# A third raw weight buffer in the down projection, operand loads of the quarter-size products on GpSimd's queue, and the seven products in another order

## The chip, the cores and the metric

The kernel runs on one core of one Trainium2 chip. The metric is the device time of one execution in microseconds (us); lower is better. Before the change three runs took 1799.60, 1798.85 and 1799.17 us, a median of 1799.17 us.

A core has five engines with instruction streams of their own, which wait for each other by semaphores: TensorE (PE, matrix products), VectorE (DVE), ScalarE (ACT), GpSimd (POOL) and SyncE (SP), which here only issues transfers (DMA). Each engine works strictly through its own list, so an instruction that waits holds back all that stand behind it.

## The reference

One step of a one-layer streaming encoder on 1056 tokens (1024 of a prompt and 32 of a sample group), in float32, with a model width of 1024: windowed attention with sinks beside a gated short convolution, cross-attention into 256 memory tokens, and a squared-ReLU MLP, each added to the residual, then a final RMS norm.

```python
x = x + (sigmoid(ga) * a + sigmoid(gb) * bo) @ w_mix_out
...
x = x + co @ w_co
hm = rms_norm(x, g_mlp)
x = x + jnp.square(jax.nn.relu(hm @ w_up)) @ w_down
...
y_prompt = rms_norm(xp, norm_final_g)
```

The change touches only the product with `w_down`, whose weight has 4096 rows and 1024 columns.

## The kernel before, in words

**Products.** Every float32 product is made from three passes of TensorE in its reduced float type: weight and operand are each split into a high part and the remainder, and high·high, high·low and low·high are added. For a weight a transfer of 512 KB brings 128x1024 values into a raw buffer `wr` (issued by SP, L164), ACT casts it to `wh` (L131), and DVE subtracts to get `wl` (L132). There are two raw buffers, and three of `wh` and of `wl`. A raw buffer is free for the next load when its `wl` is done. `next_w` keeps the casts of the two following weights issued ahead of a product (`LOOK = 2`). The third raw buffer that `fetch_w` knows (`third`, named `wr3`) is used in other parts of the kernel and is cleared before the down part.

**The down part.** It is the last 385 us. The product with `w_down` is made by a scheme of Strassen's kind: seven products of half the tokens (528) by half the depth and half the width, instead of eight. They are called b11, b21, t2, n4, n3, n1 and b22. The operand sums were written to DRAM earlier (`b_d`, `t_d`, `n_d` and so on in the trace), and for weight sums too (`wsum_d`). A product comes in one of two forms.

- `stage` (b11, t2, n3, n1, b22): eight items, each with one weight and 2 x 24 matmuls of 128x128 by 128x264 (L1923 to L1925). The results of a pair of items are added to the residual x1 by `to_x1` (L1907), 12 DVE instructions for each of four column groups in b11, 9 in t2, 6 in n3 and n1. Sixteen operands of 128x528 are loaded by SP (`fetch_op`, L1670, 264 KB each) and split by ACT (L1355) and DVE (L1356).
- `stage2` (b21 and n4): the product is divided once more into seven quarter-size products P1, P6, P2, P7, P5, P4, P3, so fourteen items of 24 matmuls (L2100 to L2102), each with one weight. Their operands are prepared during the stage before (`prepare`). For each k of eight, `fetch_two` loads two operands, POOL makes three sums (`first_sums`, L1701 to L1703), ACT and DVE split two results (`first_split`, L1708 and L1709), and later one more sum is split whole (`extra_split`, L1712 and L1713). The results are combined on ACT, DVE and POOL (L2051, L2053, L2058, L1905). At the end of a `stage2` SP loads the operands of the stage that follows: twelve transfers during its last nine items, four more with the first item of the next stage.

**What sets the order.** A scheduler places the instructions of each engine by rules of its own and by the order in which the program records them; `pin` holds an instruction at its recorded place. Stages are recorded in the order in which they are called. In a stage that comes after, or prepares, a `stage2`, the items run in the order `paired`, where two column groups advance together; in the others a column group is finished before the next begins.

**Names in the order listings.** `Ga` and `Gb` are residual tiles, `acc2` accumulators, `wl_...` remainders of a weight with a running number, `H`, `n1`, `n3`, `n4`, `t2`, `b22`, `Z`, `lt` are places for operands, and `ct` is scratch.

Of the kernel before, what the change touches and what calls it, by code (L numbers as in the profile page):

```python
# [10 lines left out]
F32 = mybir.dt.float32  # L11
# [29 lines left out]
def hybrid_step(ctx: ExitStack, tc: tile.TileContext, io):  # L41
    nc = tc.nc
    act, dve, pool_e, pe, sp = nc.scalar, nc.vector, nc.gpsimd, nc.tensor, nc.sync
# [11 lines left out]
    def closed(cm):  # L55
        cm.__exit__(None, None, None)
# [42 lines left out]
    def pin(ins):  # L99
        return tc.keep_in_program_order(ins)  # L100
# [49 lines left out]
    third = {}  # L150
# [137 lines left out]
    W = {}  # L288
# [1348 lines left out]


    dn, wanted2, coming2 = {}, [], []
    KINDS = ["b11", "b21", "t2", "n4", "n3", "n1", "b22"]  # L1640
    after2 = [KINDS[KINDS.index(kind) + 1] for kind in RAW2]


# [24 lines left out]
    def fetch_op(kind, k):  # L1668
        hi, lo = take_pair(kind, k)
        sp.dma_start(lo.bitcast(F32), op_d[kind][:, k])  # L1670
        return hi, lo
# [17 lines left out]
    two = {}  # L1689

    def fetch_two(kind, k):
        fetch_op(kind, k)
        two["x", k] = lo = take_slot((kind, 8 + k, 1))
        two["r", k] = take_slot((kind, "r", k), F32)
        sp.dma_start(lo.bitcast(F32), op_d[kind][:, 8 + k])

    def first_sums(kind, k):

# [16 lines left out]
    def extra_split(kind, k):  # L1715
        cut(*take_pair(kind, ("e", k)), two["r", k])
# [23 lines left out]
    def open_down():  # L1740
        flush()
        closed(L["cm"])
        closed(L["cm2"])
        S["h"] = ctx.enter_context(tc.tile_pool(name="hpool", bufs=1, reuse_waits="tile"))


# [72 lines left out]
    at = {}  # L1819
# [168 lines left out]
    def prepare(kind):  # L1988

        at = {n: [] for n in range(8)}  # L1990
        for n in range(4):
            for k in (2 * n, 2 * n + 1):
                at[n].append(lambda k=k: fetch_two(kind, k))
                at[n + 1].append(lambda k=k: first_sums(kind, k))
                at[n + 2].append(lambda k=k: first_split(kind, k))
        for k in range(8):
            at[6 + k // 4].append(lambda k=k: extra_split(kind, k))
        return at

    def stage(kind, w, then, q=None, each=None, more=None):  # L2000
        nxt = KINDS.index(kind) + 1
        at = prepare(KINDS[nxt]) if nxt < len(KINDS) and KINDS[nxt] in RAW2 else None
        order = paired if at or kind in after2 else steps
        if nxt < len(KINDS) and not at:
            item(lambda: wanted2.extend((KINDS[nxt], k) for k in range(16)))
        for n, (j, t) in enumerate(order):

            def fn(ws, n=n, j=j, t=t):
                prod(kind, j, t, then, q)(ws)
                if nxt < len(KINDS) and all(x[1] != t for x in order[n + 1 :]):  # L2010
                    drop_pairs(kind, range(8 * t, 8 * t + 8))
                pump2(4 if n == 0 and kind in after2 else 0 if at else 3)
                for x in at[n] if at else ():
                    x()
                if behind and (j, t) == (1, 0):
                    behind.pop()()

            item(fn, (*w, j, t))
            if each and t:
                item(lambda j=j: each(j))  # L2020
            if more and (j, t) == (1, 0):
                item(more)
        if nxt < len(KINDS):
            item(lambda: pump2(0))

    def stage2(kind, h, f0, last):
# [61 lines left out]
        n = 0  # L2088
        for p in order:
            for i in range(2):  # L2090

                def fn(w, p=p, i=i, n=n):
                    wh, wl = w
                    if i == 0 and p in start:
                        banks[into[p]] = wide_tile()
                    a = banks[into[p]][:, i, :QT]
                    for k in range(8):
                        hi, lo = operand2(kind, p, k)
                        s = slice(k * P, k * P + P)
                        pe.matmul(a, wh[:, s], hi, start=(p in start and k == 0), stop=False, skip_group_check=True)  # L2100
                        pe.matmul(a, wh[:, s], lo, start=False, stop=False, skip_group_check=True)  # L2101
                        pe.matmul(a, wl[:, s], hi, start=False, stop=(k == 7), skip_group_check=True)  # L2102
                    if i:
                        ended_with(p)
                    after(p, i)
                    beside(n)

                item(fn, weights[p](i))
                n += 1

    stage("b11", ("w_down", 0), ((*A12, True, False), (*A21, False, False), (*A22, False, False), (*A11, True, False)))
    stage2("b21", *A11, True)
    stage("t2", ("w_sum", 0), ((*A12, False, False), (*A21, True, False), (*A22, True, False)))
    stage2("n4", *A21, False)
    stage("n3", ("w_sum", 2), ((*A21, True, True), (*A22, True, False)))
    stage("n1", ("w_sum", 3), ((*A22, False, True), (*A12, True, False)), more=lambda: final(0))
    item(lambda: gained(2, range(4, 8)))
    stage("b22", ("w_sum", 1), ((*A12, True, True),), q=0)
# [121 lines left out]
```

## Time and profile before

| what | value |
|---|---|
| runs | 1799.60, 1798.85, 1799.17 us; median 1799.17 |
| the profiled execution | 1795.82 us, its span 1794.0 us, 1.82 us around it |
| PE busy | 1741.9 us (97% of the span) |
| DVE, ACT, POOL busy | 1269.9 (71%), 881.9 (49%), 756.5 us (42%) |
| loads and stores by SP's and ACT's queues | 296.37 MB, 49.7% of what 16 DMA engines could take in the span |
| by POOL's queue | 70.46 MB, 11.5% |

PE is busy nearly all the time, so the idle time of PE, and stretches in which it steps at half its clock, are what can be won. Both are concentrated in the down part, from about 1409 us on. Matmuls overlap in the trace: each is listed with 0.28 us, but the next begins 0.12 us later. At the lower clock the step is 0.22 us.

### The profile page before, as it was taken

The page shows a single profiled execution, that of the slowest core. Times are in us where ns is not written, and L with a number is a line of the kernel's source. Part 1 is how long each engine was busy: PE and PEld are TensorE (multiplying, and loading weights), DVE is VectorE, ACT ScalarE, POOL GpSimd, SP SyncE. Part 2 cuts the span into 40 slices and gives each one's busy share as a digit, 9 for nine tenths or more (in the row PEclk, how much of TensorE's full clock was granted, in tenths as well). Part 3 has the DMA queues.
Part 4 walks back from the last instruction along what each step waited for, and adds up shares of the span by engine and source line. Part 5 has one row for each costly group of instructions (what it writes and reads, how often), then busy time and mean ns, then how long its engine had stood idle before and what let it go on. Part 6 is the DMA issues. An engine that isn't in the chain of part 4 may idle for free. (4 is left out here: it accounts for less than half of the span.)

```text
span 1794.0 us, 32861 instructions
## 1 busy us (share of the span) xinstructions
PE 1741.9 (97%) x12166; PEld 1716.5 (96%) x12166; DVE 1269.9 (71%) x2322; ACT 881.9 (49%) x1716; POOL 756.5 (42%) x869
## 2 busy tenths in 40 slices
PE   9999999999999999999999999999999988989998
PEld 8999999999999999999999999999999988988998
DVE  7776877768766647646777877776666776875775
ACT  8643535435345334335565756754444444443543
POOL 0016586664664655543233240026555441731121
PEclk9999999999999999999999999999999998999999
DMA  4334445455556888877756675766666837548544
GB/s 181 108 105 139 157 162 179 162 186 177 181 182 239 293 286 281 289 253 256 260 193 212 223 241 183 271 207 216 217 221 221 315 113 227 192 132 289 195 143 156
DMA packets 191056, 369.70 MB, mean 206 GB/s; under 512 B 19616, under 2 KB 108352, under 8 KB 190768
## 3 DMA queue, kind: packets, MB, share of 16 engines
q1 hardware_dynamic: 169840, 296.37, 49.7%
q0 software_dynamic: 20432, 70.46, 11.5%
q8 instruction: 96, 1.57, 0.4%
q10 hardware_dynamic: 624, 0.77, 0.1%
q14 instruction: 64, 0.52, 0.1%
HBM read 265.41 MB, written 101.53 MB: 205 GB/s over the span
## 5 line engine op out<-in xcount | busy, mean ns | idle before, releaser
L131 ACT CAST wh<-wr 128x1024 fp32r<-128x1024 f32 (+1 forms) x226 | 236.1, 1045 | 360.9 <-PE acc L206 80.8
L132 DVE TENSOR_TENSOR wl<-wr,wh 128x1024 fp32r<-128x1024 f32 (+1 forms) x226 | 303.5, 1344 | 108.7 <-ACT wh L131 107.5
L205 PE MATMUL acc<-X,wh 128*128 128x384 f32 (+1 forms) x864 | 282.0, 326 | 0.2 <-ACT X L284 0.2
L206 PE MATMUL acc<-X,wh 128*128 128x384 f32 (+1 forms) x864 | 279.1, 323 | 0.2 <-DVE X L285 0.2
L207 PE MATMUL acc<-X,wl 128*128 128x384 f32 (+1 forms) x864 | 278.2, 322 | 0.0
L206 PEld LDWEIGHTS acc<-X,wh 128*128 128x128 f32 x864 | 162.9, 189 | 1.6 <-DVE X L285 0.5
L205 PEld LDWEIGHTS acc<-X,wh 128*128 128x128 f32 x864 | 162.6, 188 | 1.3 <-ACT X L284 0.6
L207 PEld LDWEIGHTS acc<-X,wl 128*128 128x128 f32 x864 | 162.6, 188 | 0.1
L281 POOL TENSOR_TENSOR xacc<-xacc,ct 128x384 f32<-128x384 f32 (+1 forms) x56 | 72.4, 1296 | 207.9 <-ACT ct L279 206.1
L205 PE MATMUL acc<-Y,wh 128*128 128x384 f32 (+1 forms) x432 | 140.2, 325 | 4.8 <-DVE ct L1093 3.4
L206 PE MATMUL acc<-Y,wh 128*128 128x384 f32 (+1 forms) x432 | 139.5, 323 | 0.4 <-DVE Y L816 0.4
L207 PE MATMUL acc<-Y,wl 128*128 128x384 f32 (+1 forms) x432 | 139.4, 323 | 0.4 <-DMA wl<-wl_d 0.4
L762 POOL TENSOR_TENSOR xacc<-xacc 128x256 f32<-128x256 f32 x132 | 115.0, 871 | 29.4 <-DMA xacc<-in_w_down 22.4
L762 POOL TENSOR_TENSOR ws<-ws 128x256 f32<-128x256 f32 x132 | 111.2, 842 | 26.6 <-DMA ws<-in_w_down 19.0
L131 ACT CAST PTh<-pt 128x512 fp32r<-128x512 f32 (+3 forms) x94 | 45.8, 516 | 102.2 <-PE pt L603 101.0
L205 PEld LDWEIGHTS acc<-Y,wh 128*128 128x128 f32 x432 | 81.2, 188 | 6.2 <-DVE ct L1093 4.3
L206 PEld LDWEIGHTS acc<-Y,wh 128*128 128x128 f32 x432 | 81.2, 188 | 1.0 <-DVE Y L816 1.0
L207 PEld LDWEIGHTS acc<-Y,wl 128*128 128x128 f32 x432 | 81.2, 188 | 0.7 <-DMA wl<-wl_d 0.7
L589 ACT ACTIVATE S<-S,nmx 128x257 f32<-128x257 f32 (+1 forms) x132 | 64.2, 488 | 25.7 <-DVE nmx L584 24.6
L905 PE MATMUL acc<-n,wh 128*128 128x264 f32 x256 | 72.9, 285 | 1.0 <-DVE Z L1572 1.0
L907 PE MATMUL acc<-n,wl 128*128 128x264 f32 x256 | 73.1, 285 | 0.0
L906 PE MATMUL acc<-n,wh 128*128 128x264 f32 x256 | 72.9, 285 | 0.0
(622 smaller groups left out, 5855.1 us busy)
## 6 DMA issues: line engine op xcount, KB each, us to landing
wr<-in_w_up SPq DMA_DIRECT2D x53, 512.0 KB, 4.6
wr<-in_w_in SPq DMA_DIRECT2D x52, 512.0 KB, 4.1
wr<-wsum_d SPq DMA_DIRECT2D x40, 512.0 KB, 3.5
wr<-in_w_conv_out SPq DMA_DIRECT2D x24, 512.0 KB, 4.3
wr<-in_w_mix SPq DMA_DIRECT2D x24, 512.0 KB, 4.5
wr<-in_w_down SPq DMA_DIRECT2D x20, 512.0 KB, 3.7
n_d<-Z SPq DMA_DIRECT2D x32, 264.0 KB, 4.3
xacc<-in_w_down POOLq DMA_DIRECT2D x16, 512.0 KB, 4.0
```

The lines of the kernel that those rows point to most:

```text
L131: act.copy(hi, src)
L132: dve.tensor_sub(lo, src, hi.bitcast(F32))
L205: pe.matmul(out, wh[:, a], hi, start=(k == 0), stop=False)
L206: pe.matmul(out, wh[:, a], lo, start=False, stop=False)
L207: pe.matmul(out, wl[:, a], hi, start=False, stop=(k == len(acts) - 1))
L281: pool_e.tensor_tensor(acc, acc, sq, op=ALU.add)
L589: act.activation(stl[:, h, : nk + 1], stl[:, h, : nk + 1], AF.Exp, scale=-1.0, bias=nmx[:, h : h + 1], accum_out=den[:, h : h + 1],)
L762: pin(pool_e.tensor_tensor(t[:, to], t[:, x], t[:, y], op=op))
L905: pe.matmul(acc, wh[:, a], hi, start=(start and k == 0), stop=False, skip_group_check=True)
L906: pe.matmul(acc, wh[:, a], lo, start=False, stop=False, skip_group_check=True)
L907: pe.matmul(acc, wl[:, a], hi, start=False, stop=(k == 3), skip_group_check=True)
```

## The change

Six edits, all in the down part.

1. The order of the seven products is b11, t2, b21, n3, n4, n1, b22 instead of b11, b21, t2, n4, n3, n1, b22. So b21 is prepared during t2 (before: b11) and n4 during n3 (before: t2), and each `stage2` is followed by n3 and n1 (before: t2 and n3). The marks of which addition is the last on a tile move with it, so that the sums of squares of the tiles of A21 follow n4.
2. `fetch_two` issues its two loads on POOL's queue instead of SP's, and pins them. There are 16 of them in each preparation, 32 in all.
3. `open_down` gives `fetch_w` a third raw buffer, in memory that is free by then; every third weight of the down part goes there.
4. The eight calls of `extra_split` are spread over three items as 2, 3, 3 instead of over two as 4, 4; so those of k = 0, 1 and 4 are recorded one item earlier.
5. In `stage2`, the casts of the next weight are recorded directly after the matmuls of an item, ahead of that item's combinations and splits (`issue_w()`), so one weight further ahead.
6. The calls at the end stand in the new order.

```diff
-    KINDS = ["b11", "b21", "t2", "n4", "n3", "n1", "b22"]
+    KINDS = ["b11", "t2", "b21", "n3", "n4", "n1", "b22"]
...
     def fetch_two(kind, k):
-        fetch_op(kind, k)
+        pin(pool_e.dma_start(take_pair(kind, k)[1].bitcast(F32), op_d[kind][:, k]))
         two["x", k] = lo = take_slot((kind, 8 + k, 1))
         two["r", k] = take_slot((kind, "r", k), F32)
-        sp.dma_start(lo.bitcast(F32), op_d[kind][:, 8 + k])
+        pin(pool_e.dma_start(lo.bitcast(F32), op_d[kind][:, 8 + k]))
...
         closed(L["cm2"])
+        third.update(n=0, pool=W["pool"])
...
         for k in range(8):
-            at[6 + k // 4].append(lambda k=k: extra_split(kind, k))
+            at[5 + (k + 1) // 3].append(lambda k=k: extra_split(kind, k))
...
                         pe.matmul(a, wl[:, s], hi, start=False, stop=(k == 7), skip_group_check=True)
+                    issue_w()
                     if i:
                         ended_with(p)
                     after(p, i)
...
     stage("b11", ("w_down", 0), ((*A12, True, False), (*A21, False, False), (*A22, False, False), (*A11, True, False)))
+    stage("t2", ("w_sum", 0), ((*A12, False, False), (*A21, True, False), (*A22, True, False)))
     stage2("b21", *A11, True)
-    stage("t2", ("w_sum", 0), ((*A12, False, False), (*A21, True, False), (*A22, True, False)))
-    stage2("n4", *A21, False)
-    stage("n3", ("w_sum", 2), ((*A21, True, True), (*A22, True, False)))
+    stage("n3", ("w_sum", 2), ((*A21, True, False), (*A22, True, False)))
+    stage2("n4", *A21, True)
     stage("n1", ("w_sum", 3), ((*A22, False, True), (*A12, True, False)), more=lambda: final(0))
```

Lines of the changed kernel are numbered one higher from L1742 on, and two higher from L2104 on.

**DVE's list in the first half of b11.** Each `acc2` is one column group's accumulator, and its 12 additions stand between its first and its last row here. Before:

```order
L132 TENSOR_TENSOR wl_3055_17362<-wr_3053_17359,wh_3054_17361 128x1024
L1907 TENSOR_TENSOR Ga1_1910_10779<-acc2_3044_17290,Ga1_1910_10779 128x240
...
L1907 TENSOR_TENSOR Ga1_1910_10779<-acc2_3044_17290,Ga1_1910_10779 128x144
L1907 TENSOR_TENSOR Ga1_1935_10868<-acc2_3056_17365,Ga1_1935_10868 128x240
...
L1907 TENSOR_TENSOR Ga1_1935_10868<-acc2_3056_17365,Ga1_1935_10868 128x144
L132 TENSOR_TENSOR wl_3071_17447<-wr_3069_17444,wh_3070_17446 128x1024
```

Now:

```order
L132 TENSOR_TENSOR wl_3053_17359<-wr_3051_17356,wh_3052_17358 128x1024
L1908 TENSOR_TENSOR Ga1_1910_10779<-acc2_3044_17290,Ga1_1910_10779 128x240
...
L1908 TENSOR_TENSOR Ga1_1910_10779<-acc2_3044_17290,Ga1_1910_10779 128x144
L1356 TENSOR_TENSOR H_3046_17348<-H_3046_17348,H_3045_17347 128x528
L1356 TENSOR_TENSOR H_3048_17351<-H_3048_17351,H_3047_17350 128x528
L1356 TENSOR_TENSOR H_3050_17354<-H_3050_17354,H_3049_17353 128x528
L132 TENSOR_TENSOR wl_3062_17440<-wr3_3060_17437,wh_3061_17439 128x1024
...
L1908 TENSOR_TENSOR Ga1_1935_10868<-acc2_3063_17443,Ga1_1935_10868 128x240
...
L1908 TENSOR_TENSOR Ga1_1935_10868<-acc2_3063_17443,Ga1_1935_10868 128x144
L132 TENSOR_TENSOR wl_3074_17520<-wr_3072_17517,wh_3073_17519 128x1024
```

Two groups of 12 additions stood in a row without a weight between them; now a weight's remainder, and three more splits behind it, stand between the two groups. The name `wr3` shows the third buffer in use.

**DVE's list at the passage into b21**, from the remainder for its second item (P1, second half) on. Before, at the end of b11:

```order
L132 TENSOR_TENSOR wl_3118_17851<-wr_3116_17848,wh_3117_17850 128x1024
L1907 TENSOR_TENSOR Gb1_1967_10999<-acc2_3104_17709,Gb1_1967_10999 128x240
...
L1907 TENSOR_TENSOR Gb1_1967_10999<-acc2_3104_17709,Gb1_1967_10999 128x144
L1713 TENSOR_TENSOR n1_3120_17915<-n4_3077_17530,n1_3119_17914 128x528
L1713 TENSOR_TENSOR n1_3122_17919<-Z_3081_17536,n1_3121_17918 128x528
L1713 TENSOR_TENSOR n1_3124_17923<-Z_3090_17624,n1_3123_17922 128x528
L1713 TENSOR_TENSOR n1_3126_17927<-lt_3094_17630,n1_3125_17926 128x528
L132 TENSOR_TENSOR wl_3129_17933<-wr_3127_17930,wh_3128_17932 128x1024
```

Now, at the end of t2:

```order
L132 TENSOR_TENSOR wl_3180_18410<-wr_3178_18407,wh_3179_18409 128x1024
L1908 TENSOR_TENSOR Gb1_1967_10999<-Gb1_1967_10999,acc2_3164_18267 128x240
...
L1908 TENSOR_TENSOR Gb2_2339_12584<-acc2_3164_18267,Gb2_2339_12584 128x264
L1713 TENSOR_TENSOR H_3182_18471<-n3_3141_18097,H_3181_18470 128x528
L1713 TENSOR_TENSOR n4_3184_18475<-b22_3150_18182,n4_3183_18474 128x528
L1713 TENSOR_TENSOR n4_3186_18479<-b22_3154_18188,n4_3185_18478 128x528
L132 TENSOR_TENSOR wl_3189_18485<-wr_3187_18482,wh_3188_18484 128x1024
L132 TENSOR_TENSOR wl_3193_18516<-wr3_3191_18513,wh_3192_18515 128x1024
```

The remainder for P6's first half (`wl_3129`, now `wl_3189`) stood behind 12 additions and 4 splits; now it stands behind 9 and 3, and the one for P6's second half follows at once.

**SP's list in the second half of n4**, where `wr_3377` and `wr_3382` (now `wr_3433` and `wr3_3441`) are the weights of P4 and the two after them those of P3. Before:

```order
L164 DMA wr_3377_19465<-in_w_down 128x4x256
L164 DMA wr_3382_19504<-in_w_down 128x4x256
L1670 DMA t2_3374_19460<-n3_d_100 128x528
L1670 DMA t2_3376_19463<-n3_d_100 128x528
L1670 DMA n1_3387_19539<-n3_d_100 128x528
L1670 DMA n1_3389_19542<-n3_d_100 128x528
L1670 DMA H_3399_19615<-n3_d_100 128x528
L164 DMA wr_3390_19544<-w2_n4_106 128x4x256
```

Now:

```order
L164 DMA wr_3433_19998<-in_w_down 128x4x256
L1670 DMA b22_3428_19936<-n1_d_99 128x528
L164 DMA wr3_3441_20036<-in_w_down 128x4x256
L164 DMA wr_3445_20074<-w2_n4_106 128x4x256
L1670 DMA H_3437_20006<-n1_d_99 128x528
L1670 DMA H_3439_20009<-n1_d_99 128x528
L1670 DMA H_3450_20085<-n1_d_99 128x528
L1670 DMA n4_3452_20088<-n1_d_99 128x528
L1670 DMA t2_3464_20167<-n1_d_99 128x528
L164 DMA wr_3453_20114<-w2_n4_106 128x4x256
```

P3's first weight stood behind five operand loads of the next stage; now it stands ahead of them, and only P3's second weight is behind five.

On POOL's list the preparation now runs by pairs of k: four loads, the six sums of these, the next four loads, the next six sums, and so on through four pairs; before, the sums stood in a row and their loads were all on SP. On PE's list the first half of P2 is now split into pieces, between which the second half of P6 and the first half of P7 stand, and 18 matmuls of the next stage stand ahead of P3's second half, which before came first. The counts of matmuls and of DVE and ACT instructions are the same in both kernels.

## The prediction

> **What bounds the kernel now.** I read the page first (PE busy 97%), then the table of stretches for the down part, one row for each of the first six products.
>
> ```profile
> core 0: us, PE busy (x) PEld busy (x) DVE busy (x) ACT busy (x) POOL busy (x), PEclk, DMA share, GB/s
> 1408.70:1470.90 62.20, 56.31 (x434) 55.26 (x433) 47.87 (x84) 28.77 (x51) 32.12 (x31) 0.95 0.66 231
> 1470.90:1528.90 58.00, 47.68 (x338) 45.84 (x337) 40.47 (x59) 26.05 (x38) 16.86 (x18) 0.91 0.64 206
> 1528.90:1580.50 51.60, 49.61 (x386) 48.56 (x385) 40.31 (x66) 23.69 (x43) 31.66 (x32) 0.97 0.47 163
> 1580.50:1638.00 57.50, 47.92 (x339) 45.97 (x338) 42.13 (x56) 25.16 (x35) 17.20 (x17) 0.91 0.67 212
> 1638.00:1687.10 49.10, 48.21 (x386) 47.05 (x386) 32.41 (x52) 22.96 (x35) 5.02 (x5) 1.00 0.66 220
> 1687.10:1734.80 47.70, 47.70 (x394) 47.70 (x393) 34.64 (x65) 23.16 (x40) 7.13 (x5) 1.00 0.51 161
> ```
>
> The sixth row (n1) is a stage without a gap: 394 matmuls in 47.70 us, a step of 0.121. By that step an ordinary stage of 384 takes 46.5 us and a quarter-size product (14 x 24 = 336) 40.7. So b21 and n4 (second and fourth row) lose 58.0 + 57.5 - 81.4 = 34 us, t2 5, n3 2.6, and b11 9 to 10 after some 50 matmuls of the up product (434 - 384, 6 us) are taken off: about 51 us in all, the ceiling of any gain. Who is waited for stands in the table of waits, 1400 to 1700 us (us in total, times, longest):
>
> ```profile
> PE acc L2102 <- DVE wl L132: 12.1, 7, 3.2
> PE acc L1925 <- DVE wl L132: 5.6, 4, 4.1
> PE acc L2100 <- ACT wh L131: 2.7, 2, 1.4
> SPq L164 <- DVE wl L132: 106.4, 28, 12.2
> ```
>
> PE waits for weights, 20.4 us in these rows; SP's loads wait for the subtraction that frees a raw buffer. The chain of waits of 1470 to 1530 says how:
>
> ```profile
> 1479.61 1.15 DVE wl L132
> 1480.78 4.21 DMA wr<-in_w_down
> 1485.06 1.05 ACT wh L131
> 1486.14 1.24 DVE wl L132
> 1487.39 3.49 DMA wr<-w_b
> ...
> 1509.07 6.16 DMA wr<-w_b
> 1515.33 1.05 ACT wh L131
> 1516.40 1.24 DVE wl L132
> ```
>
> It begins with a remainder on DVE that comes late (what stands ahead of it follows below), and from there the loop of a raw buffer carries the time: load, cast, remainder, next load. A loop takes 3.49 + 1.05 + 1.24 = 5.8 us undisturbed and 6.16 + 1.05 + 1.24 = 8.5 while operands are loaded. Two buffers give a weight each 2.9 to 4.2 us; an item needs one each 24 x 0.122 = 2.93. PE's own rows show the stalls this leaves, and the clock behind them:
>
> ```profile
> 1445.28 0.59 PE L1925 MATMUL acc<-t,wl 128*128 128x264 f32 x1 [4.05 <-DVE wl L132]
> 1445.66 0.43 PE L1923 MATMUL acc<-t,wh 128*128 128x264 f32 x1
> ...
> 1450.50 0.29 PE L1924 MATMUL acc<-t,wh 128*128 128x264 f32 x1
> 1480.81 0.39 PE L2102 MATMUL acc<-t,wl 128*128 128x264 f32 x1 [3.18 <-DVE wl L132]
> 1501.98 0.59 PE L2102 MATMUL acc<-b,wl 128*128 128x264 f32 x1 [2.53 <-DVE wl L132]
> 1516.42 0.39 PE L2100 MATMUL acc<-n,wh 128*128 128x264 f32 x1 [1.32 <-ACT wh L131]
> 1517.68 0.39 PE L2102 MATMUL acc<-n,wl 128*128 128x264 f32 x1 [0.75 <-DVE wl L132]
> 1589.42 0.39 PE L2102 MATMUL acc<-Z,wl 128*128 128x264 f32 x1 [2.15 <-DVE wl L132]
> 1610.81 0.51 PE L2102 MATMUL acc<-t,wl 128*128 128x264 f32 x1 [2.53 <-DVE wl L132]
> ```
>
> After the stall of 4.05 us, 21 steps of 0.22 us follow before they are 0.12 again, 0.098 more each: 2 us. After each of the others of 2 us and more, and after the pair of 1.32 and 0.75, I count 11 to 14 such steps in the same view, 1.1 to 1.4 us; grouped, they are the mean clock of 0.91 in the rows of b21 and n4.
>
> **The change, part by part.** The sum is made against the profiled execution, 1795.82 us, which lies 3.35 below the median of 1799.17.
>
> *Order of products, in b11.* The 4.05 us at 1445.28 are a remainder behind two groups of 12 additions on DVE. Now the remainder stands between the groups; a group takes 3.0 us (1474.09 to 1477.06 in the rows below), so with three splits it is ready long before two items (2 x 48 x 0.122 = 11.7 us) are over. That saves 4.05 + 2.0 = 6.1. The splits that came in lie in DVE's idle time: two items now hold 12 additions (3.0), two remainders of 1.24 (2.5) and six splits of 0.69 (4.1), 9.6 of 11.7 us. I take -5.6.
>
> *Passage into the quarter-size products.* DVE's rows ahead of the 3.18 us stall:
>
> ```profile
> 1468.22 3.06 DVE L1713 TENSOR_TENSOR t<-H,t 128x528 fp32r<-128x528 f32 x3
> 1472.39 1.77 DVE L132 TENSOR_TENSOR wl<-wr,wh 128x1024 fp32r<-128x1024 f32 x1
> 1474.09 0.82 DVE L1907 TENSOR_TENSOR Gb<-acc,Gb 128x240 f32<-128x240 f32 x3
> 1477.06 0.69 DVE L1713 TENSOR_TENSOR n<-n,n 128x528 fp32r<-128x528 f32 x1
> ```
>
> Before b21, two blocks of 12 additions and 4 splits become two of 9 and 3: 2 x 3 x 0.25 = 1.5 us of additions and 1.04 + 0.62 of splits less, 3.1 of the 3.18. Before n4 nine additions become six, again 1.5, and two splits less, 1.7: all of the 2.15. With the slow steps behind both (27 x 0.098 = 2.6) that is 7.9 at most, and half of it if POOL slows DVE there (a remainder there took 1.77 at 1472.39, and 1.24 in the chain). I take -6.6.
>
> *Third raw buffer, operand loads off SP's list, earlier casts.* They answer one thing, the loop. With three buffers the loop of 5.8 to 8.5 us gives a weight each 1.9 to 2.8 us, under 2.93 at both ends. P5's weight (2.53 at 1501.98) can be loaded one remainder earlier, about one item (2.9 us); P3's (1.32 + 0.75) no longer stands behind five operand loads. The same two stalls in n4 are 2.53 and, with the waits for `wh` and `wl` left in the table, 2.1. Together 9.3, and 52 slow steps behind them (5.1): 14.4 at most. Not all can go: the transfers themselves don't shrink, and casts still wait for one of three `wh`. At the other end a late load costs each `stage2` half of what it does now, 5 of 14.4. I take one stall of 1.3 with its clock 0.7 left in each, so -10.4.
>
> The Trainium skill ("TensorE: Matmul & The Clock Gate", the part on what is actually happening) has the clock fall only after an idle window of about 3.4 us; the trace disagrees, since stalls of 2.15 and 2.53 us also brought slow steps. By the page the 1.4 us of clock that I leave here would fall away, and the sum would be 1.4 us lower.
>
> *Operands of the stage after.* The preparation and the first splits of freshly loaded operands met in t2, and the splits were late while POOL was at work:
>
> ```profile
> 1542.81 0.39 PE L1924 MATMUL acc<-b,wh 128*128 128x264 f32 x1 [0.55 <-DVE b L1356]
> 1545.68 0.39 PE L1925 MATMUL acc<-Z,wl 128*128 128x264 f32 x1 [0.82 <-DVE wl L132]
> ```
>
> That meeting now falls on n3, so these stalls and the slow steps behind them (clock 0.97 in t2's row), some 3.5 of t2's 5 us, go, and n3's loss grows as much, while n1 takes n3's: +0.7 net, from 0 to +2.
>
> *Refill.* After a stall the first step is 0.16 longer than the next (0.38 from 1445.28 to 1445.66, then 0.22); nine stalls fewer are -1.4.
>
> *What is new.* 32 loads on POOL, the chain of sums behind them, and 18 matmuls of the next stage ahead of P3's second half, which needs operands that are loaded last. Rows for POOL, the third of them from b11 alone, the last from 1470 to 1530 us:
>
> ```profile
> L1702 POOL TENSOR_TENSOR n<-ct,n 128x264 f32<-128x264 f32 x5 | 5.3, 1068 | 0.4
> L1702 POOL TENSOR_TENSOR H<-ct,H 128x264 f32<-128x264 f32 x3 | 3.8, 1276 | 0.2
> L1702 POOL TENSOR_TENSOR n<-ct,n 128x264 f32<-128x264 f32 x2 | 1.5, 765 | 0.2
> L739 POOL DMA_DIRECT2D ws<-in_w_down x16 | 9.4, 585 | 12.6 <-DMA wsum_d<-ws 12.6
> ws<-in_w_down POOLq DMA_DIRECT2D x16, 512.0 KB, 3.8
> n<-n_d SPq DMA_DIRECT2D x6, 264.0 KB, 6.3
> ```
>
> A load costs POOL 0.585 us, 18.7 for all, on an engine that is busy 32 of 52 us at most. But loads and sums now alternate: two loads (1.2), landing (3.8), six sums (6.4, or 4.6 at 0.765) make a pair of 9.6 to 11.4, four pairs 38 to 46 us. They must be done about when the preparing stage ends (46.5) and P1's first item has run (2.9): 49. So it is hidden; without that cover each us over costs a us. For the 18 matmuls and the pieces of P2 I take +3 (0 to +6: a stall of 2.15 with its clock in each `stage2` is nearest).
>
> Sum: -5.6 - 6.6 - 10.4 + 0.7 - 1.4 + 3 = -20.3; 1775.5 for the profiled execution, 1778.9 for the median: **1779 us**, 1.1% faster.
>
> **The rivals.**
>
> *All weight stalls vanish* (-6.1 - 7.9 - 14.4 - 2.9 of refill, nothing new): -31.3, 1768. For it speaks n1, where PE runs without a gap; against it that the transfers of n4's end (two of three weights beside twelve operand loads) stay as many.
>
> *DVE takes the place of the raw buffers.* DVE is busy 40.5 and 42.1 us in the two quarter-size products, which could last 40.7: its work alone is as long as PE's. If every remainder then comes late behind splits and combinations, the two stay near 55.5 us: b11's 5.6 and 2 x 2 are won, 0.7 lost, 1790. Against it: in the chain DVE's other work stands only up to 1479, and after that the loads.
>
> *Slower: POOL's chain overruns.* A pair with the slow landing of 6.3 and sums of 1.276 is 1.2 + 6.3 + 7.7 = 15.2 us, four are 61, 12 over the cover of 49. P1 then waits for its last splits and P6 for its extra ones: twice 12 us, and some 1.4 us of clock each, +27 against a gain of 20.3: 1806. It decides from pairs of 12.2 us (49 / 4) on, and eats the whole gain at 14.5. Against it: the slow landings stand where SP's weights and twelve operand loads crowd, not in the preparing stages (DMA share 0.47 in t2).
> The Trainium skill ("SBUF — State Buffer", the box on DVE blocking DMA) has the descriptors of GpSimd's loads written by GpSimd itself, which is locked out while DVE runs certain copies: 3.1 us instead of 0.62 for a small one. So far the trace speaks against it: POOL's loads of 512 KB landed in 3.8 us, SP's in 3.49 to 6.16 in the chain. By the page's difference of 2.5 us a pair would be 12 to 14, an estimate that lands on this rival's threshold.
>
> *It doesn't do what it says* (the third buffer stays unused): excluded for the buffer by the name `wr3` in the order; a gain of b11 alone, cancelled by new waits, would be within 0.2%.
>
> **How the numbers follow.** My forecast (1770 to 1790) 0.60; all stalls gone (below 1770) 0.10; DVE the bound (1790 to 1795.6) 0.10; no change 0.07; slower 0.13, of which POOL's chain 0.10. 0.2%, about what a measurement of this kernel can tell, is 3.6 us: faster is below 1795.6. So faster 0.80, same 0.07, slower 0.13. The range for 8 in 10 goes from 1766 (the first rival and 2 us) to 1797, where DVE's case ends and no change begins.
>
> **What would show it.** Right: no gap of 4 us in b11; in both quarter-size products no row of PE waiting over 1.5 us for `wl` L132, stretches of 47 to 51 us (before 58.0 and 57.5), granted clock over 0.95 there; SP's wait for `wl` well below 106 us. Wrong in the third term: P5 and P3 still wait for `wh` or `wl`, with the load just landed. DVE's rival: the same waits with the raw data long there, the chain running through DVE. POOL's rival: PE waits in the first item of b21 and n4 for L1709 or L1713, and these for POOL L1703. The forecast fails altogether if new waits appear in the stages that were clean (n1, b22) or the tail.

## The result, and the profile after

The changed kernel takes 1775.85 us (median of four runs, 1772.86 to 1778.70) against 1799.01 us for the kernel before on the same chip: a ratio of 0.9872, 95% interval 0.9853 to 0.9890. The forecast was 1779 us. Run beside other kernels later it took 1777.01 us, ratio 0.9879 (0.9856 to 0.9901). The profiled execution took 1777.22 us, its span 1775.4, so it gained 18.6 us on the profiled execution of before; the medians differ by 23.2.

The table of stretches, cut at the first matmul of each of the first six products in their new order, b11, t2, b21, n3, n4, n1 (columns as before). After b21 and n4, 18 matmuls of the next stage stand ahead of P3's second half; there the cut lies 18 steps of 0.122 us ahead of the matmul behind P3, so that these 18 count with their own stage:

```profile
core 0: us, PE busy (x) PEld busy (x) DVE busy (x) ACT busy (x) POOL busy (x), PEclk, DMA share, GB/s
1408.50:1466.45 57.95, 55.02 (x434) 54.39 (x433) 43.42 (x82) 28.14 (x43) 12.23 (x13) 0.97 0.82 284
1466.45:1513.23 46.78, 46.78 (x387) 46.78 (x385) 30.67 (x68) 17.79 (x32) 24.18 (x35) 1.00 0.48 152
1513.23:1563.48 50.25, 44.33 (x339) 41.59 (x337) 36.34 (x52) 25.53 (x36) 18.46 (x18) 1.00 0.71 230
1563.48:1610.22 46.74, 46.74 (x387) 46.74 (x385) 29.50 (x43) 20.58 (x37) 32.70 (x41) 1.00 0.58 185
1610.22:1668.16 57.94, 47.09 (x338) 44.39 (x337) 44.35 (x64) 29.85 (x45) 27.84 (x26) 0.91 0.61 202
1668.16:1715.92 47.76, 47.76 (x394) 47.76 (x393) 40.15 (x69) 27.88 (x50) 10.68 (x9) 1.00 0.66 226
```

t2 and n3 now run without a gap, at full clock. b21 went from 58.0 to 50.3 us. But n4 takes 57.9, as long as before, at a mean granted clock of 0.91: one of the two quarter-size products won nothing. The table of waits of PE over the down part says why:

```profile
PE acc L2102 <- DVE lt L1709: 6.1, 1, 6.1
PE acc L2103 <- DVE wl L132: 2.5, 7, 0.6
PE acc L1925 <- DVE n L1356: 2.5, 2, 1.4
PE acc L1926 <- DVE wl L132: 2.0, 3, 0.8
PE acc L1924 <- ACT wh L131: 1.1, 1, 1.1
```

PE's waits for weights (`wl` and `wh`) fell from 20.4 us to 5.6, none of them longer than 1.1 us. In their place stands one wait of 6.1 us, for a first split (L1709). PE's rows show where, in n4's first item, and a second wait behind it, for an extra split:

```profile
1619.14 0.59 PE L2102 MATMUL acc<-lt,wh 128*128 128x264 f32 x1 [6.08 <-DVE lt L1709]
1621.19 0.59 PE L2102 MATMUL acc<-b,wh 128*128 128x264 f32 x1 [1.03 <-DVE b L1713]
```

25 slow steps of 0.22 us come with it (2.4 us). The split that PE waits for comes late on DVE's list:

```profile
1610.73 0.43 DVE L1709 TENSOR_TENSOR Z<-Z,n 128x264 fp32r<-128x264 f32 x1 [5.93 <-POOL lt L1702]
1612.00 1.57 DVE L1908 TENSOR_TENSOR Gb<-acc,Gb 128x264 f32<-128x264 f32 x6
...
1616.44 1.75 DVE L132 TENSOR_TENSOR wl<-wr,wh 128x1024 fp32r<-128x1024 f32 x1
1618.12 0.97 DVE L1709 TENSOR_TENSOR lt<-lt,b 128x264 fp32r<-128x264 f32 x1
```

DVE stood idle for 5.93 us, waiting for POOL's sums (L1702). Then six additions of n3's last result, three extra splits and a weight's remainder, 6.1 us from 1612.00 to 1618.12, stood ahead of the split that PE needed. What DVE waited for is on POOL's list, from its timeline:

```profile
1567.48 1.81 POOL L1906 TENSOR_TENSOR Ga<-ct,Ga 128x120 f32<-128x120 f32 x2 [1.60 <-DVE ct L2059]
1569.23 0.57 POOL L1692 DMA_DIRECT2D H<-n_d  x1
...
1575.53 1.28 POOL L1701 TENSOR_TENSOR ct<-H,H 128x264 f32<-128x264 f32 x1 [2.89 <-DMA H<-n_d]
...
1603.32 0.55 POOL L1692 DMA_DIRECT2D Z<-n_d  x1
...
1609.12 0.75 POOL L1701 TENSOR_TENSOR ct<-n,Z 128x264 f32<-128x264 f32 x1 [3.63 <-DMA n<-n_d]
...
1613.60 1.18 POOL L1703 TENSOR_TENSOR Z<-b,Z 128x264 f32<-128x264 f32 x1
```

POOL's chain for n4 begins at 1569.23, 5.8 us after n3 has begun by the cut above, because additions of b21's results (L1906, the last at 1567.48) stand ahead of it. Its pairs begin at 1569.2, 1582.5, 1592.4 and 1603.3, and the last sum ends at 1614.8: pairs of 13.3, 9.9, 10.9 and 11.5 us. n4 began at 1610.2. The same chain for b21 had ended 17.7 us before b21 began (1513.23). It could start during b11, with its first load at 1458.48, and it took 37.0 us:

```profile
1462.29 1.32 POOL L1701 TENSOR_TENSOR ct<-t,t 128x264 f32<-128x264 f32 x1 [1.53 <-DMA t<-b_d]
...
1494.66 0.82 POOL L1703 TENSOR_TENSOR b<-b,b 128x264 f32<-128x264 f32 x1
```

### The profile page after: what moved, and what is told of

Its sections match the earlier page's. It is cut to its first block, busy times and chain, and to the rows that moved or that the text cites. A ratio compares the mean times of both kernels' runs of the same rounds, so it can differ in the third digit from the quotient of the medians.

```text
span 1775.4 us, 32859 instructions
## 1 busy us (share of the span) xinstructions
PE 1733.3 (98%) x12166; PEld 1708.7 (96%) x12166; DVE 1256.8 (71%) x2322; ACT 882.4 (50%) x1716; POOL 773.2 (44%) x901
## 3 DMA queue, kind: packets, MB, share of 16 engines
q1 hardware_dynamic: 165232, 287.71, 48.9%
q0 software_dynamic: 22992, 79.12, 13.3%
## 5 line engine op out<-in xcount | busy, mean ns | idle before, releaser
L132 DVE TENSOR_TENSOR wl<-wr,wh 128x1024 fp32r<-128x1024 f32 (+1 forms) x226 | 296.3, 1312 | 99.7 <-ACT wh L131 98.7
```

Of the source, the lines that this page charges most:

```text
L132: dve.tensor_sub(lo, src, hi.bitcast(F32))
```

## The experiments

**How they are compared.** Whole runs of one kernel spread over up to 13 us here. Most of that lies ahead of the part that is changed: the down part's first matmul came anywhere from 1403 to 1416 us in the profiles, with the same instructions ahead of it. So beside the median of the runs I give the length of the **down part** in the one profile, from the start of that matmul to the end of the span: 1794.0 - 1408.7 = 385.3 us before, 366.9 for the changed kernel and 365.5 when it ran again. The last two are the only pair of profiles of one kernel, and say that one profile stands for the kernel within some 1 to 2 us. The stages by themselves, cut as above:

| kernel | median us (same chip, before) | ratio, 95% interval | down part | b11 | b21 | t2 | n3 | n4 |
|---|---|---|---|---|---|---|---|---|
| before | 1799.01 | | 385.3 | 62.2 | 58.0 | 51.6 | 49.1 | 57.4 |
| changed | 1775.85 (1799.01) | 0.9872, 0.9853 to 0.9890 | 366.9 | 57.9 | 50.2 | 46.8 | 46.7 | 57.9 |
| changed, again | 1777.01 (1798.85) | 0.9879, 0.9856 to 0.9901 | 365.5 | 56.4 | 48.7 | 46.8 | 47.3 | 59.1 |
| third buffer alone | 1780.04 (1796.03) | 0.9895, 0.9864 to 0.9925 | 371.1 | 62.3 | 53.7 | 46.8 | 46.7 | 54.6 |
| order alone | 1789.55 (1796.03) | 0.9959, 0.9940 to 0.9979 | 382.6 | 58.1 | 57.0 | 46.8 | 53.0 | 59.3 |
| earlier casts alone | 1794.61 (1798.85) | 0.9977, 0.9958 to 0.9995 | 384.9 | 62.6 | 57.3 | 51.3 | 51.0 | 55.8 |
| changed, two buffers | 1789.90 (1796.03) | 0.9960, 0.9938 to 0.9982 | 379.9 | 58.0 | 55.3 | 46.8 | 48.9 | 61.7 |
| changed, no earlier casts | 1782.05 (1798.85) | 0.9900, 0.9873 to 0.9926 | 367.8 | 58.0 | 50.4 | 46.8 | 46.7 | 58.8 |
| changed, loads on SP | 1772.19 (1798.85) | 0.9855, 0.9818 to 0.9892 | 358.8 | 58.0 | 49.3 | 46.8 | 49.1 | 48.8 |
| changed, loads ahead of sums | 1770.66 (1796.03) | 0.9850, 0.9827 to 0.9873 | 359.0 | 58.0 | 49.1 | 46.8 | 47.3 | 51.0 |
| order and third buffer | 1778.12 (1800.53) | 0.9882, 0.9848 to 0.9915 | 361.3 | 57.6 | 51.8 | 46.8 | 46.7 | 51.6 |
| order, buffer, earlier casts | 1772.55 (1800.53) | 0.9851, 0.9817 to 0.9884 | 361.0 | 58.0 | 52.3 | 46.8 | 47.0 | 50.1 |
| loads ahead, one cast earlier | 1772.28 (1800.53) | 0.9856, 0.9816 to 0.9895 | 365.8 | 58.6 | 51.3 | 46.8 | 46.7 | 55.5 |
| loads on SP, one cast earlier | 1773.59 (1800.53) | 0.9859, 0.9819 to 0.9898 | 360.1 | 57.7 | 49.7 | 46.8 | 49.1 | 49.9 |

n1 took 47.7 to 49.3 us, b22 47.9 to 48.0 and what follows 11.2 to 12.0 in all of them.

### The third raw buffer alone

```diff
         closed(L["cm2"])
+        third.update(n=0, pool=W["pool"])
```

> The kernel before with one edit: the third raw buffer in the down part. Theory A (the loop of load, cast and remainder held back the weights of the quarter-size products): the stalls before P5 and P3 and the slow steps behind them go, up to 14.4 us; the 4.05 us in b11 and the stalls of P6 stay, since these are DVE's list. So 10 to 14 us faster, 1785 to 1789 us. Rival B (the order of the products on DVE's list is what counts): at most 3 us faster. Rival C (the third buffer alone is the change): about 20 us faster, 1779 us.

The down part fell by 14.2 us, the median by 16. That is theory A's size or a little over it, and rival B falls. But the gain doesn't lie where A had put it: P5's stall of 2.53 us is still there in both products. DVE's timeline of this kernel before the stall in b21, with ACT's cast of that weight and PE's row:

```profile
1499.41 0.43 DVE L1908 TENSOR_TENSOR Ga<-acc,Ga 128x264 f32<-128x264 f32 x1 [3.09 <-PE acc L2103]
1499.76 0.70 DVE L1713 TENSOR_TENSOR n<-n,H 128x528 fp32r<-128x528 f32 x1
1500.37 0.70 DVE L1713 TENSOR_TENSOR Z<-n,n 128x528 fp32r<-128x528 f32 x1
1500.99 2.35 DVE L132 TENSOR_TENSOR wl<-wr,wh 128x1024 fp32r<-128x1024 f32 x2
```

```profile
1496.47 1.06 ACT L131 CAST wh<-wr 128x1024 fp32r<-128x1024 f32 x1 [0.96 <-PE acc L2102]
```

```profile
1502.26 0.40 PE L2103 MATMUL acc<-b,wl 128*128 128x264 f32 x1 [2.53 <-DVE wl L132]
```

The weight was cast by 1497.5. Its remainder stands on DVE behind the addition of P2's result (L1908), which waits 3.09 us for PE to finish P2's second half, and behind two splits. The same stands in the trace of before, in DVE's timeline; the piece of the chain that the prediction read there was the transfer that follows:

```profile
1499.12 0.43 DVE L1907 TENSOR_TENSOR Ga<-acc,Ga 128x264 f32<-128x264 f32 x1 [2.92 <-PE acc L2102]
...
1500.70 2.35 DVE L132 TENSOR_TENSOR wl<-wr,wh 128x1024 fp32r<-128x1024 f32 x2
```

What the buffer did bring: P3's stalls of 2.1 us each are gone, with waits of 1.5 and 0.75 us for the next stage's first weight in their place, and t2 and n3 take 4.8 and 2.4 us less, no longer than a stage without a gap.

### The order of the products alone

```diff
-    KINDS = ["b11", "b21", "t2", "n4", "n3", "n1", "b22"]
+    KINDS = ["b11", "t2", "b21", "n3", "n4", "n1", "b22"]
```

with the calls at the end in that order.

> The kernel before with one edit: the new order of the seven products. Theory A: b11's stall of 4.05 us and P6's two stalls shrink with their slow steps, 10 to 13 us, while P5 and P3 still wait for weights: 1786 to 1789 us. Rival B: about 20 us faster. Rival C: at most 3 us faster.

b11 fell by 4.1 and t2 by 4.8 us, as the changed kernel's did. Still the down part fell by only 2.8 us, because n3 and n4 grew by 5.8 (49.1 + 57.4 to 53.0 + 59.3): with two raw buffers, PE waits for weights at the end of the quarter-size products and in n3. The table of waits of this kernel:

```profile
PE acc L2102 <- DVE wl L132: 9.5, 6, 2.5
PE acc L2100 <- ACT wh L131: 5.4, 4, 2.3
```

The median gained 6.5 us, still under the 10 to 13 expected. With the preparation of n4, t2's loss moved to n3, as the prediction had it: t2 51.6 to 46.8, n3 49.1 to 53.0.

### The changed kernel with two raw buffers

The line of `open_down` that sets `third` is left out.

> The changed kernel without the third raw buffer. Theory A: the stalls before P5 and P3 come back, so 8 to 14 us slower than the changed kernel, about 1784 to 1790 us, with PE waiting for L131 and L132 over 1.5 us there. If the other edits (operand loads off SP's list, earlier casts) already break the loop, as rival B has it: within 3 us of the changed kernel.

13.0 to 14.4 us longer in the down part than the two profiles of the changed kernel: as theory A has it, at its upper end. By the medians, each against the kernel before on its own chip, it is 15.7 to 17.0 (a gain of 6.1 instead of 21.8 to 23.2). The largest loss isn't at P5 or P3, but a stall of 9.22 us in n4 after P1's first half. ACT's timeline there:

```profile
1623.29 1.04 ACT L131 CAST wh<-wr 128x1024 fp32r<-128x1024 f32 x1 [9.53 <-DMA wr<-w_n]
1624.24 0.37 ACT L2051 COPY n<-acc 128x264 f32<-128x264 f32 x1
```

and the chain of waits that leads to it:

```profile
1601.84 5.91 DMA b<-n_d
...
1609.62 0.72 DVE lt L1709 x2
...
1613.34 1.49 DVE Gb L1907 x6
...
1618.27 1.69 DVE wl L132
...
1619.98 3.24 DMA wr<-w_n
```

The chain comes from POOL again: the last of its loads landed at 1607.8, which made DVE late with the splits. So the remainder that frees a raw buffer ended at 1620, the next load could only then begin, and ACT stood 9.5 us at its cast with the copy of P1's result behind it. In the changed kernel, with a third buffer, POOL is late too, but there no cast waits for a weight's load. So part of what the buffer is worth here is cover for POOL's lateness, which the kernel before doesn't have.

### POOL's loads ahead of the sums

In the changed kernel POOL waits for each pair's landing. Here `prepare` records the four loads of a pair ahead of the six sums of the pair before:

```diff
-                at[n].append(lambda k=k: fetch_two(kind, k))
+                at[n].insert(k % 2, lambda k=k: fetch_two(kind, k))
```

> The changed kernel with one thing moved: in the preparation, POOL issues the four loads of a pair before the six sums of the pair ahead of it, not after, so that a landing lies under sums. In the changed kernel PE waits 6.1 us for the last splits of n4, and 1.0 us more, with 25 slow steps behind (2.4 us). Theory D (POOL's chain of loads, landings and sums is what is late there, each landing adds 2 to 4 us to it): the stall goes or shrinks below 1 us, 7 to 9.5 us faster than the changed kernel, 1766 to 1769 us. Rival E (the chain is late because it starts 10 us after n3 does, and the loads wait for places that PE frees, so that pulling them up only makes POOL wait earlier): under 3 us gained, the stall in n4 stays over 4 us.

Theory D holds. POOL's rows for n4 in this kernel, whose n3 began at 1559.7 and n4 at 1606.9:

```profile
1566.04 0.56 POOL L1692 DMA_DIRECT2D H<-n_d  x1
...
1599.44 0.95 POOL L1701 TENSOR_TENSOR ct<-b,lt 128x264 f32<-128x264 f32 x1
```

No sum waits for a landing now. The last sums are done by 1602.2, 4.7 us before n4 begins, instead of 4.6 after. The stall of 6 us is gone, n4 takes 51.0 us instead of 57.9, and the down part 359.0 instead of 365.5 to 366.9. The start was as late as before (6.4 us after n3's), so the start alone doesn't make the stall, and rival E falls. PE still waits 2.28 us for a remainder before P6 in n4.

### The changed kernel again

> The changed kernel once more, beside the three that follow, as their standard: 1772 to 1779 us, as before. Its stall of 6 us in the first item of n4 should be there again if POOL's chain is late by its own length, and gone or halved if it was an accident of one execution.

The stall was there again, 5.82 us at the same place. It belongs to the kernel.

### The earlier casts, alone and taken away

```diff
+                    issue_w()
                     if i:
                         ended_with(p)
```

> The kernel before with one edit: in the quarter-size products the casts of the next weight are recorded directly after an item's matmuls. With the third buffer alone, P5's stall of 2.53 us stayed in both products though its weight had landed and was cast 3.5 us before: its remainder stood on DVE behind the addition of P2's result, which waits for PE. Theory A2 (P5's stalls come from DVE's list, P3's from the raw buffers): both stalls of P5 go with some 24 slow steps, 5 to 8 us faster than before, 1788 to 1792 us by this chip's time; P3's stay. Theory A as predicted (P5 waits for the raw buffer): both stay, at most 2 us faster.

> The changed kernel without that edit. Theory A2: P5's stall of about 2.5 us is back in both products, 5 to 8 us slower than the changed kernel. Theory A as predicted: the third buffer has removed it, within 2 us of the changed kernel.

On the cause of P5's stalls A2 holds: added to the kernel before, the edit removes both, and taken out of the changed kernel it brings both back. PE's rows of the latter, in b21 and n4:

```profile
1545.56 0.39 PE L2103 MATMUL acc<-lt,wl 128*128 128x264 f32 x1 [2.54 <-DVE wl L132]
1545.79 0.29 PE L2101 MATMUL acc<-lt,wh 128*128 128x264 f32 x1
1545.91 0.29 PE L2102 MATMUL acc<-lt,wh 128*128 128x264 f32 x1
...
1651.45 0.39 PE L2103 MATMUL acc<-H,wl 128*128 128x264 f32 x1 [2.53 <-DVE wl L132]
```

On the size A2 was wrong: the down part moved by 0.4 us in the one and by 0.9 to 2.3 in the other, not by 5 to 8. The traces show why. In the kernel with two buffers the loop of the raw buffer only moves its wait. P3's waits in its first half, which A2 expected to stay, are gone; instead PE waits 1.75 us (b21) and 2.34 us (n4) for a combination on DVE (L2058) ahead of P3's second half, where 0.83 stood before. That combination stands on DVE behind a remainder whose cast waited 1.74 and 3.18 us for its load. And n3 grew by 1.9 us. In the changed kernel without the edit both stalls came back, but at full clock: the rows behind the first follow at steps of 0.12 us, where the same stall in the kernel before was followed by steps of 0.22:

```profile
1501.98 0.59 PE L2102 MATMUL acc<-b,wl 128*128 128x264 f32 x1 [2.53 <-DVE wl L132]
1502.36 0.43 PE L2100 MATMUL acc<-b,wh 128*128 128x264 f32 x1
1502.58 0.43 PE L2101 MATMUL acc<-b,wh 128*128 128x264 f32 x1
```

The medians moved by 4.2 and 5.0 us. With one profile of each, the runs don't settle whether the edit is worth that or the 0.4 to 2.3 of the down part.

### The operand loads on SP's queue again

```diff
-        pin(pool_e.dma_start(take_pair(kind, k)[1].bitcast(F32), op_d[kind][:, k]))
+        fetch_op(kind, k)
...
-        pin(pool_e.dma_start(lo.bitcast(F32), op_d[kind][:, 8 + k]))
+        sp.dma_start(lo.bitcast(F32), op_d[kind][:, 8 + k])
```

> The changed kernel with the operand loads of the quarter-size products on SP's queue again, as before the change. Theory D (POOL's alternation of loads and sums makes n4 late): the stall of 6 us goes, 5 to 9 us faster than the changed kernel, 1767 to 1771 us. Theory F (SP's list was a bottleneck, and moving the loads off it was needed even with three buffers): weights come late in the preparing stages t2 and n3, stalls on L131 and L132 there, 3 us slower than the changed kernel or more.

The down part took 358.8 us, 6.7 to 8.1 less than the changed kernel's, and the median was 4.8 less than that of the changed kernel run beside it (1777.01), though the two intervals of the ratio overlap. Its rows for n3 and n4:

```profile
1570.05:1619.11 49.06, 47.97 (x387) 47.00 (x385) 41.77 (x59) 24.97 (x45) 31.81 (x31) 1.00 0.54 184
1619.11:1667.90 48.79, 44.22 (x339) 41.70 (x337) 36.13 (x48) 25.57 (x36) 19.47 (x20) 1.00 0.72 234
```

n4 is 9.1 us shorter than in the changed kernel and at full clock; n3 is 2.3 longer. Theory D holds and F falls: SP's list with the loads costs something in n3, but a quarter of what POOL's chain costs in n4. With three raw buffers the move to POOL's queue was a loss. The other profiles agree: the four kernels with the new order, three buffers and the loads on SP's queue have down parts of 358.8 to 361.3 us, and those with POOL's loads in turn with the sums 365.5 to 367.8.

### The order and the third buffer together

> The kernel before with two edits: the third raw buffer and the new order of products. Measured by the down part, from its first matmul to the end of the span: 385.3 us before, 371.1 with the third buffer alone, 382.6 with the order alone. Theory G (the order's gain on DVE's list, about 11 us by the stalls that it removes in b11 and before P6, was eaten by weights that came late with two raw buffers): 360 to 362 us, 9 to 11 less than with the buffer alone. Rival H (the two remove the same stalls, so little is added): 367 to 370 us.

361.3 us, as theory G has it. The order takes 9.8 us off the kernel with three buffers (371.1) and 2.8 off the one with two (382.6 from 385.3); the buffer takes 14.2 off the old order and 21.3 off the new one. By these profiles, one of each kernel, each is worth 7 us more with the other. The medians don't show it: against the kernel before beside them they gain 16.0 and 6.5 us alone and 22.4 together. Their intervals, 3.5 to 6 us to either side, are too wide to exclude it.

### The order, the buffer and the earlier casts

> The same and the earlier casts in the quarter-size products: everything of the change except the loads on POOL's queue and the spread of the extra splits. P5's stall of 2.5 us should go in both products. Down part 358 to 360 us; the changed kernel with loads on SP's queue has 358.8, so the spread of the extra splits would be worth under 1 us. If the spread matters: 361 us or more, with the stall before P6 back.

361.0 us: the earlier casts are worth 0.3 on top. P5's stalls went, but two waits for remainders of 1.4 to 1.5 us take their place, and one of 1.4 before P6 in b21 stays; the kernel that also spreads the extra splits and is otherwise the same (loads on SP) has none of the three and takes 358.8. That is the other of the two outcomes named: the spread is worth about 2 us, near what two profiles of one kernel differ by.

### One more cast ahead, in the last item before a quarter-size product

```diff
             part(bank[j], w, kind, t)
+            if early:
+                issue_w()
```

with `early` true for the eighth item of a stage that prepares a quarter-size product; once on the kernel with loads ahead of sums, once on the one with loads on SP.

> The kernel with the operand loads of a pair ahead of the sums of the pair before it (down part 359.0 us), and one more weight cast recorded ahead of the residual additions' follow-up splits in the last item before a quarter-size product. There PE still waits 2.28 us for a remainder in n4, with 1.5 us of slow steps behind it. If the remainder behind three splits on DVE is the cause: 355 to 357 us. If the early cast only waits for one of the three cast buffers and holds ACT's list: no gain, 359 us or more.

> The same early cast in the changed kernel with operand loads on SP's queue (down part 358.8 us). That kernel has no wait for a remainder above 0.8 us in n4, so by the same theory nothing is to be had: 358 to 360 us.

No gain: 365.8 us where 355 to 357 were expected (in the slowest of the four runs, which is the profiled one), and 360.1 for the second, within what was expected of it. The wait before P6 in n4 grew from 2.28 to 3.40 us. ACT's timeline:

```profile
1616.41 1.05 ACT L131 CAST wh<-wr 128x1024 fp32r<-128x1024 f32 x1 [3.38 <-PE acc L1925]
1617.36 0.63 ACT L1712 CAST n<-Z 128x528 fp32r<-128x528 f32 x1
```

The early cast waits 3.38 us for PE to give one of the three `wh` free, and the casts for the extra splits stand behind it. That is the second outcome. The runs' median (1772.28) is that of the kernel without it within their spread, so by whole runs I can't call it a loss.

The two kernels with loads on SP or loads ahead of sums beat both the kernel before and, by 7 us of the down part and about 5 us of the medians, the changed one. Which of them is better the runs don't tell.

## Why the prediction was right or wrong

The time and the direction were right: 1779 us forecast, 1775.85 measured, inside the range of 1766 to 1797. For the profiled execution it was 1775.5 against 1777.22. That the sum came out so near was luck: two errors of about 8 us offset each other. Going by the down part, b21 and n4 together were to win 15.4 (-6.6 - 10.4 - 1.4 + 3) and won 7.3 (115.5 to 108.2), and t2, n3 and n1 were to lose 0.7 and won 7.1.

- **b11, -5.6.** Measured -4.3 (62.2 to 57.9). The 4.05 us are gone as said. What was not seen: the waits at b11's own last splits grew, from four of 0.36 to 0.55 us at 1427 to 1432 to two of 1.36 and 1.10 for L1356 and one of 0.47, with 12 slow steps. Every profile with the new order has the two.
- **Passage into the quarter-size products, -6.6.** In b21 right: 3.18 us became 0.16. In n4 2.15 us became a wait of 1.03 for an extra split, behind the larger stall.
- **Third raw buffer, loads off SP's list, earlier casts, -10.4.** I had these answer one thing, the loop of the raw buffer. They answer three. The buffer is worth 14.2 us alone and 13.0 to 14.4 in the changed kernel, as large as the upper bound of 14.4 that I gave all three. P5's stalls, 5.06 of the 9.3 us in that term, were not the loop but DVE's list, and it was the earlier casts that removed them, worth 0.4 to 2.3 us by the down part and 4 to 5 by the medians. And the loads off SP's list are a loss of 6.7 to 8.1 us.
- **Operands of the stage after, +0.7.** This is the step that failed most on the other side. I let t2's loss of 3.5 us move to n3 with the preparation. With the order alone it does; in the changed kernel it went nowhere: t2, n3 and n1 took 51.6 + 49.1 + 47.7 = 148.4 us before and 46.8 + 46.7 + 47.8 = 141.3 after, -7.1. With the third buffer alone t2 is just as clean (46.8), although the preparation and the fresh operands still meet there. So POOL slowing the splits was not what held t2 up; the two raw buffers were. The traces of the two kernels show the step. Before, in t2:

```profile
1536.87 1.05 ACT L131 CAST wh<-wr 128x1024 fp32r<-128x1024 f32 x1 [3.43 <-DMA wr<-wsum_d]
```

```profile
1537.95 1.26 DVE L132 TENSOR_TENSOR wl<-wr,wh 128x1024 fp32r<-128x1024 f32 x1 [2.80 <-ACT wh L131]
```

The splits that PE waits for stand on DVE behind this remainder, which waits for a cast that waits for its load. With the third buffer alone the casts at that place wait for PE and not for a load, and these splits begin 4.7 us after t2 does instead of 10.2, though they still take up to 1.25 us each.
- **Refill, -1.4.** Not measured by itself.
- **What is new, +3.** POOL's chain was costed as hidden, with 38 to 46 us against a cover of 49. The chain's length was right: 45.6 us in n4. The cover was not: in n4 it starts 5.8 us after n3, behind b21's last additions on POOL. It cost 6.08 + 1.03 of stalls and 2.4 of slow steps, 9.5 us. The price was wrong too: "each us over costs a us" would give the 2 to 3 us by which the chain overran, but DVE, which had stood idle for POOL, had 6.1 us of other work on its list ahead of the last split. The 18 matmuls of the next stage ahead of P3's second half, which I took the +3 for, cost 1.9 and 0.9 us, waits for that stage's first weight. They come with the third buffer: the kernel with the buffer alone has them, the changed kernel with two buffers doesn't.

The rivals: the first (all weight stalls vanish, 1768) describes the profile of PE best apart from n4; the kernels with loads ahead of sums and on SP's queue come nearest to it, with 25.4 and 26.7 us less than the kernel before beside them against its 31.3. The slower rival's mechanism happened, in one product of two, with pairs of 11.4 us in the mean: the late start leaves 49 - 5.8 = 43 us of cover, so it decides from pairs of 10.8 us on and not from 12.2. Its price of 27 was far off, since b21's chain started early and so cost nothing. The Trainium skill's warning ("SBUF — State Buffer", the box on DVE blocking DMA) isn't what struck: POOL's loads are issued in 0.55 us each and landed in 3.1 to 6.8 us in n3 (medians by tile), while the same loads took 6.1 to 7.0 from SP's queue in the kernel that has them there. POOL waits 1.6 to 3.6 us for the first landing of each pair, and changing the order on the same queue removed those waits. DVE's rival is out for b21, where PE's longest wait for a remainder of its own weights is 0.5 us.

One sign that the prediction named for being right failed. SP's wait for `wl` was to fall well below 106 us; it rose to 148.7:

```profile
SPq L164 <- DVE wl L132: 148.7, 37, 12.9
```

PE's waits for weights fell in the same profile from 20.4 to 5.6 us, so SP's wait is no measure of what PE loses.

On the clock, the stalls of 6.08 and 1.03 us were followed by 25 slow steps, and those of 1.36 and 1.10 us in b11 by 12. The Trainium skill ("TensorE: Matmul & The Clock Gate", what is actually happening) gives an idle window of about 3.4 us as the condition; b11's case did without one. But the prediction, which adds slow steps to every stall of 2 us or more, was wrong as well. The two stalls of 2.53 and 2.54 us in the changed kernel without the earlier casts had none. Nor had b11 in the second profile of the changed kernel, after the same waits (1.35, 1.11 and 0.50 us); its b11 took 56.4 us instead of 57.9, 1.5 us less, as much as the two profiles differ by. What decides, no run here shows.

## What to carry to other kernels

Before moving transfers to a less busy engine, write down what stands on its list between them. Here each load that POOL issued and then consumed turned its landing into idle time of POOL (1.6 to 3.6 us a pair) and, through DVE's list, into 6 us of idle time of PE. These waits went away when the next loads were issued ahead of the work on the last. A wait put down to a weight, `wl` here, has two possible causes, its buffer or the list of the engine that makes it, and the timeline of that engine (what it waited for just before) tells them apart where the chain of waits doesn't. Two edits that remove waits from the same path can be worth more together than apart, so a small gain of one alone says little: here, by one profile of each kernel, 2.8 us became 9.8 once the buffer was there, though the medians don't show it.

## What the runs showed that I had not expected

The whole-run time of one and the same kernel spread over up to 13 us between executions (1791.25 to 1804.13 for the kernel before in one series), and the profiles put most of it ahead of the changed part: the down part began between 1403 and 1416 us and then took 365.5 and 366.9 us in two executions of the changed kernel. Comparing a stretch between two fixed instructions gave a resolution of 1 to 2 us, where the medians gave 4.
